# Value products of a two-layer mixer: operands built on chip from both parts of x, values kept on chip, layer 1's value sums made in layer 0, residual rows finished late

## The chip, the core and the metric

The kernel runs on one core of a Trainium2 chip. The metric is the device time of one execution in microseconds, as the median of several runs. The engines named below each work through a queue of their own in order: PE (TensorE) multiplies matrices, DVE (VectorE) and ACT (ScalarE) work elementwise, POOL (GpSimd) does elementwise work and issues DMAs, SP (SyncE) only issues DMAs.

## What is computed

Two layers of one mixer. Each layer projects x (512 tokens by 2048) with one wide weight matrix, runs three groups of attention heads, multiplies each group's output with a gate, projects back and normalises.

```python
def hybrid_layer(x, mem, w_in, b_forget, w_mem_kv, w_out, ln_gain, ln_bias):
    h = jnp.einsum('bsd,dn->bsn', x, w_in)
    (fq, fk, fv, fg, f_logit, dq, dk, dv, dg, iq, ik, iw, mq, mg) = jnp.split(h, offsets, axis=-1)
    log_f = jax.nn.log_sigmoid(f_logit + b_forget)
    y_fox = fox_attention(heads(fq), heads(fk), heads(fv), jnp.cumsum(log_f, axis=1)) * silu(fg)
    y_dsa = dsa_attention(rope(heads(dq)), rope(heads(dk)), heads(dv), rope(iq), rope(ik), iw) * silu(dg)
    k_mem, v_mem = jnp.split(jnp.einsum('bmd,dn->bmn', mem, w_mem_kv), 2, axis=-1)
    y_mem = memory_attention(heads(mq), k_mem, v_mem) * silu(mg)
    y = jnp.einsum('bsn,nd->bsd', jnp.concatenate([y_fox, y_dsa, y_mem], axis=-1), w_out)
    return layer_norm(ALPHA * x + y, ln_gain, ln_bias)      # x of the next layer

def reference(x, ...):
    for l in range(2):
        x = hybrid_layer(x, mem, w_in[l], ...)
    return x
```

There are 6 fox heads, 6 sparse (dsa) heads and 4 memory heads of width 128. The values fv and dv together are 1536 columns.

## The kernel before

All matrix products are made in float32r with every operand split in a high and a low part (`split`: ACT rounds the high part, DVE subtracts it to get the low part), and each product is three matmuls: high by high, low by high, high by low (`product`, L198 to L200).

**The weight stream.** The weights are a list of chunks of 1 MB (`wall`). One chunk after another is loaded by SP into one of three buffers `raw` (`load_w`, L214), split by halves into `whi` and `wlo` (`split_w`, three half chunks ahead of PE), and used by PE. A chunk is 48 matmuls of 512 columns for most kinds, and 24 of them for a chunk of the memory projection or of a value product. The load of chunk i+2 stands in SP's queue at the start of chunk i, behind all that was written into that queue before.

**Order.** The main loop goes over the chunks: memory values (mv), memory keys (mk), queries and gates of the memory heads (mq, mg), values, small columns, indexer queries, then per head gate, query and key, the third column block of the values (val, j = 2) between the fox and the dsa heads, and the output projection. All other work is written as generators: `begin(gen)` starts one, and `tick()` lets each running generator write its next piece, twice per chunk. What a generator writes stands in the engines' queues at that place.

**Values.** The first two thirds of the value columns, and the output projection, are made as a 2 by 2 block product with 7 instead of 8 block products (`PRODUCTS`, `VAL_ORDER`: P1, P2, Q6, P7, Q5, Q4, Q3). Their right operands are weight blocks or sums of them, T1 to T4. These sums are made in device memory by POOL's DMAs, copies and accumulating copies of 1 MB (`weight_sums`), sixteen DMAs for the values of one layer; before each, DVE writes a mark that POOL reads (`pool_waits`), so that the DMA is issued at the place in time at which it is written. The left operands are blocks of x or sums of them, S1 to S4: block (t, kh) is token half t and half kh of the 2048 inputs. Before the change they are made from x in device memory: `load_vx` has SP load twenty 256 KB blocks per layer (from `xt_in` for layer 0; for layer 1 from `xt_d`, into which `next_x` has SP store the new x, L783), DVE adds or subtracts 512 columns at once, and `val_operand` splits the sum at once. The finished values (`val_out`) are stored to device memory by SP (`v_d`, L724), eight tiles per layer for j = 0 and 1, and loaded again at head 0 and 4 (`load_v`, L729).

**Between the layers.** `next_x` normalises the sixteen tiles z (DVE), transposes them (PE, L779), scales and splits them (ACT L781 and L784; DVE and POOL L786). That runs beside mv and mk of layer 1. Later it has POOL multiply each z with the gain row, add the bias row and store the tile to `x1_d` as the residual of layer 1 (L796 to L798), beside the memory heads of layer 1.

**Buffers.** One pool of 69 tiles of 128 by 512 holds nearly everything else (`slot`), and PSUM has 8 banks.

Of the kernel before, what the change touches and what calls it, by code (L numbers as in the profile page):

```python
# [150 lines left out]
def kernel(  # L151
# [156 lines left out]
    def weight_sums(kind, l, pairs, names, pause):  # L308
# [4 lines left out]
        for name in names:  # L313
            for n, step in enumerate(steps[name]):
                for pair, g in every:
# [11 lines left out]
                    yield pause  # L327

    crow_d = [dram.tile([H_FOX, SEQ], F32, name=f"crow{l}") for l in range(DEPTH)]
    x1_d = dram.tile([SEQ, DM], F32, name="x1")  # L330
    v_d = {(j, st): dram.tile([P, 512], F32, name=f"v{j}{st}") for j in range(2) for st in range(4)}
    xt_d = dram.tile([P, KT * SEQ], F32, name="xt1")
# [336 lines left out]
    def val_operands(l):  # L669
        first = ((0, 0), (1, 0), (1, 1))  # L670
        load_vx(l, 0, *first)
        yield 1
        for i in range(4):
            if i < 3:
                load_vx(l, i + 1, *first)
            a11, a21, a22 = (vx.pop((*b, i)) for b in first)
            nc.vector.tensor_tensor(a21, a11, a21, op=ALU.subtract)
            nc.vector.tensor_tensor(a22, a21, a22, op=ALU.add)
            vx["S3", i], vx["S2", i] = a21, a22
            yield 1  # L680
            val_operand("S2", i, a22)
            yield 1
        for i in range(4):
            load_vx(l, i, (0, 0))
            val_operand("S3", i, vx.pop(("S3", i)))
            yield 1
        for i in range(4):
            load_vx(l, i, (0, 1))
            t = vx.pop((0, 0, i))
            nc.vector.tensor_tensor(t, t, vx["S2", i], op=ALU.subtract)  # L690
            val_operand("S1", i, t)
            yield 1
        for i in range(4):
            t = vx.pop((0, 1, i))
            nc.vector.tensor_tensor(t, t, vx.pop(("S2", i)), op=ALU.subtract)
            val_operand("S4", i, t)
            yield 2
# [10 lines left out]
    def val_out(name, ps):  # L708

        if name in ("P1", "P7", "Q6"):  # L710
# [44 lines left out]

    def load_rows(l):
        for c in range(4):
            for name, src in (("g", gain), ("b", bias)):
                t = slot("row")
                nc.gpsimd.dma_start(t, bass.AP(tensor=src.tensor,  # L760
                                               offset=src.offset + l * DM + c * 512,
                                               ap=[[0, P], [1, 512]]))
                rows[name, c] = t
# [4 lines left out]
    def next_x():  # L768
# [6 lines left out]
        for k in range(KT):  # L775
# [7 lines left out]
            nc.sync.dma_start(xt_d[:, k * SEQ:(k + 1) * SEQ], xf)  # L783
# [6 lines left out]
        yield 6  # L790
        load_rows(0)
        yield 2
# [7 lines left out]
        rows.clear()  # L800
# [71 lines left out]
    for i, (kind, l, j, col, _) in enumerate(chunks):  # L872
# [130 lines left out]
        elif kind == "val" and col == 3:  # L1003
            for st in range(4):
                vraw[j, st] = slot("vraw")
                nc.scalar.activation(vraw[j, st], out_ps[st], AF.Copy)
# [32 lines left out]
        if i == (8 if l == 0 else first[l]):  # L1039
            begin(weight_sums("val", l, range(1), ("T1", "T2", "T3", "T4"), 1 + l))  # L1040
        if kind == "mg" and j == H_MEM - 2:
            begin(val_operands(l))
        if kind == "small":
            chains.clear()
            begin(weight_sums("out", l, range(2), ("T1", "T3", "T2", "T4"), 2))
        if kind in ("fk", "dk"):
            n = j if kind == "fk" else H_FOX + j
            if n % 4 == 0:
                begin(split_v(n // 4))
        if kind == "fq" and j % 4 == 0:  # L1050
# [100 lines left out]
```

## Time and profile before

| what | value |
|---|---|
| median of 3 runs (lowest, highest) | 2005.66 us (2003.26, 2006.2) |
| the profiled execution's own time | 2005.69 us |
| its span from the first to the last instruction | 2003.9 us |
| mean granted TensorE clock | 0.994 |
| busy: PE, DVE, ACT, POOL | 1960.8, 1340.5, 780.5, 276.0 us |
| bytes read and written in device memory | 367.02 MB, 119.56 MB |

The profile is read from the whole to the part: the share of each engine, then what the bound engine waited for and where, then the queues of the engines that it waited for. A row of waits reads: engine, tile and line that waited, what released it, and then the total in us, the number of waits and the longest. A row of a timeline reads: start in us, duration in us, engine, line, operation, tiles, and in brackets the idle time before it and what ended that. Where several equal instructions are merged, x gives their number.

### The profile page before, as it was taken

How to read it: one execution, taken by the hardware profiler on the slowest of the kernel's cores; microseconds unless marked ns; L12 is line 12 of the kernel's file. 1: busy time of each engine (PE TensorE's matmuls, PEld its weight loads, DVE VectorE, ACT ScalarE, POOL GpSimd, SP SyncE). 2: the span in 40 equal slices, each digit the busy share in tenths (PEclk: the TensorE clock that was granted, in tenths of full speed). 3: DMA queues.
4: the chain of work that ended last, by engine and by line, in shares of the span. 5: the costliest groups of instructions: out<-in, count | busy, mean ns of one | idle time of the engine just before them, and what ended most of it. 6: DMA issues, size and time to landing. Idle time of an engine off the chain costs nothing. (4 is left out here: it accounts for less than half of the span.)

```text
span 2003.9 us, 24622 instructions
## 1 busy us (share of the span) xinstructions
PE 1960.8 (98%) x9410; PEld 1662.9 (83%) x9410; DVE 1340.5 (67%) x2205; ACT 780.5 (39%) x1232; POOL 276.0 (14%) x447
## 2 busy tenths in 40 slices
PE   9999999999999999999979999999999999999997
PEld 8887798888888888888868877988888888888886
DVE  6447577667864566788835675776678745657888
ACT  6334334433322332445453343344333223324453
POOL 0110011121110000100135610111221100001101
PEclk9999999999999999999989999999999999999999
DMA  9797559555664222466498974595656652224766
GB/s 368 242 300 234 200 197 269 165 167 178 169 193 143 85 84 84 163 221 228 160 299 294 263 252 176 213 266 163 181 168 179 183 144 92 77 83 168 279 208 154
DMA packets 72305, 385.41 MB, mean 192 GB/s; under 512 B 8688, under 2 KB 18928, under 8 KB 37884
## 3 DMA queue, kind: packets, MB, share of 16 engines
q1 hardware_dynamic: 57116, 262.18, 36.3%
q0 software_dynamic: 15072, 121.67, 23.4%
q8 instruction: 73, 1.20, 0.2%
q14 instruction: 44, 0.36, 0.1%
HBM read 367.02 MB, written 119.56 MB: 243 GB/s over the span
## 5 line engine op out<-in xcount | busy, mean ns | idle before, releaser
L192 DVE TENSOR_TENSOR wlo<-raw,whi 128x1024 fp32r<-128x1024 f32 (+1 forms) x425 | 523.0, 1236 | 244.7 <-ACT whi L191 243.3
L198 PE MATMUL c<-xh,whi 128*128 128x512 f32 (+1 forms) x1696 | 650.2, 383 | 0.4 <-ACT whi L191 0.4
L200 PE MATMUL c<-xh,wlo 128*128 128x512 f32 (+1 forms) x1696 | 647.0, 382 | 0.5 <-DVE wlo L192 0.5
L199 PE MATMUL c<-xl,whi 128*128 128x512 f32 (+1 forms) x1696 | 646.5, 381 | 0.0
L191 ACT ACTIVATE whi<-raw 128x1024 fp32r<-128x1024 f32 (+1 forms) x425 | 443.4, 1052 | 314.4 <-PE z L200 74.0
L200 PEld LDWEIGHTS c<-xh,wlo 128*128 128x128 f32 x1696 | 318.3, 188 | 57.9 <-DVE wlo L192 1.0
L198 PEld LDWEIGHTS c<-xh,whi 128*128 128x128 f32 x1696 | 318.5, 188 | 55.8 <-ACT whi L191 0.8
L199 PEld LDWEIGHTS c<-xl,whi 128*128 128x128 f32 x1696 | 318.6, 188 | 55.0
L199 PE MATMUL z<-wlo,yh 128*128 128x512 f32 (+1 forms) x434 | 167.8, 387 | 1.2 <-DVE wlo L192 1.2
L198 PE MATMUL z<-whi,yh 128*128 128x512 f32 (+1 forms) x434 | 167.9, 387 | 0.0
L200 PE MATMUL z<-whi,yl 128*128 128x512 f32 (+1 forms) x434 | 167.6, 386 | 0.0
L306 POOL TENSOR_TENSOR seen<-mark,mhalf 128x1 f32<-128x1 f32 x96 | 31.1, 323 | 863.8 <-DVE mark L305 759.9
L199 PEld LDWEIGHTS z<-wlo,yh 128*128 128x128 f32 x434 | 81.5, 188 | 18.2 <-DVE wlo L192 2.1
L198 PEld LDWEIGHTS z<-whi,yh 128*128 128x128 f32 x434 | 81.5, 188 | 16.4
L200 PEld LDWEIGHTS z<-whi,yl 128*128 128x128 f32 x434 | 81.5, 188 | 16.4
L198 PE MATMUL v<-whi,xh 128*128 128x512 f32 x224 | 87.6, 391 | 0.0
L191 ACT ACTIVATE qh<-rope 128x512 fp32r<-128x512 f32 x24 | 15.2, 633 | 185.1 <-DVE rope L427 185.1
L200 PE MATMUL v<-whi,xl 128*128 128x512 f32 x224 | 87.2, 389 | 0.0
L199 PE MATMUL v<-wlo,xh 128*128 128x512 f32 x224 | 87.2, 389 | 0.0
L191 ACT ACTIVATE qh<-c 128x512 fp32r<-128x512 f32 x32 | 19.2, 598 | 146.8 <-PE c L200 141.9
L191 ACT ACTIVATE pth<-pt 128x512 fp32r<-128x512 f32 (+1 forms) x72 | 35.3, 526 | 100.5 <-PE pt L590 98.6
L424 DVE TENSOR_TENSOR rope<-c,tabs 128x512 f32<-128x512 f32 (+2 forms) x42 | 26.8, 639 | 69.0 <-PE c L200 68.7
(193 smaller groups left out, 2697.1 us busy)
## 6 DMA issues: line engine op xcount, KB each, us to landing
raw<-in_wall_dram SPq DMA_DIRECT2D x163, 1024.0 KB, 7.1
sum<-in_wall_dram POOLq DMA_DIRECT2D x48, 1024.0 KB, 8.9
raw<-sum SPq DMA_DIRECT2D x48, 1024.0 KB, 5.0
vx<-in_xt_dram SPq DMA_DIRECT2D x20, 256.0 KB, 11.0
vx<-xt SPq DMA_DIRECT2D x20, 256.0 KB, 6.7
memraw<-in_memt_dram SPq DMA_DIRECT2D x16, 256.0 KB, 5.9
xraw<-in_xt_dram SPq DMA_DIRECT2D x16, 256.0 KB, 9.1
v<-vraw SPq DMA_DIRECT2D x16, 256.0 KB, 2.2
```

The source lines that it names most:

```text
L191: nc.scalar.activation(hi, src, AF.Copy)
L192: nc.vector.tensor_tensor(lo, src, hi.bitcast(F32), op=ALU.subtract)
L198: nc.tensor.matmul(ps, ah, bh, start=start, stop=False, skip_group_check=more)
L199: nc.tensor.matmul(ps, ah, bl, start=False, stop=False, skip_group_check=more)
L200: nc.tensor.matmul(ps, al, bh, start=False, stop=stop, skip_group_check=more)
L306: nc.gpsimd.tensor_tensor(seen, mark, mhalf, op=ALU.mult)
L424: nc.vector.tensor_tensor(t1[:rows, c], ps[:rows, c], cos[:rows, c], op=ALU.mult)
```

## The change

The left operands of the value products are now made from the parts of x that are on chip already, the tiles `xh` and `xl` (`val_sum`): a sum of two blocks is the two high parts and the two low parts, added one after another on DVE in pieces of 256 columns, 80 instructions for one layer. `val_operand` writes the high part, and the low part only at the next tick. The sums S1 and S2 are made from mq 0 on; S3 beyond the first tile waits until P1 is done, the splits of S1 until Q6 is done, those of S4 until P7 is done. `load_vx`, the store of x in `next_x` and `xt_d` are gone. The values of j = 0 and 1 stay on chip; those of j = 2 are stored and loaded instead (at dk 2), and `split_v(1)` begins at fq 4, one chunk earlier. The value sums of layer 1 follow the output sums of layer 0 in one generator (`sums_ahead`), and the value sums of layer 0 have longer pauses. `next_x` stores z as it is, and `residual_rows` reads each tile again, finishes it on POOL and stores it, beside the third value block and the first dsa heads of layer 1.

```diff
@@ load_w
-            src = wall[key] if kind == "wall" else sums.pop(key)
+            src = wall[key] if kind == "wall" else sums[key]
@@ weight_sums
-                    yield pause
+                    yield next(pauses) if pauses else 2
+    def value_sums(l, pauses=None):
+        return weight_sums("val", l, range(1), ("T1", "T2", "T3", "T4"), pauses)
+    def sums_ahead(l):
+        yield from weight_sums("out", l, range(2), ("T1", "T3", "T2", "T4"))
+        if l + 1 < DEPTH:
+            yield from value_sums(l + 1)
@@ the left operands
-    def load_vx(l, i, *blocks):
-        src = (xt_in if l == 0 else xt_d).rearrange("p (k t c) -> p k t c", k=KT, t=2)
-        for t, kh in blocks:
-            vx[t, kh, i] = slot("vx")
-            nc.sync.dma_start(vx[t, kh, i].rearrange("p (k c) -> p k c", k=2),
-                              src[:, 8 * kh + 2 * i:8 * kh + 2 * i + 2, t, :])
-    def val_operand(name, i, x):
-        vleft[name, i] = slot("vxh", F32R), slot("vxl", F32R)
-        split(x, *vleft[name, i])
...
+    def x_block(t, kh, i, e, part):
+        return xT[8 * kh + 2 * i + e][part].bitcast(F32)[:, t * 256:(t + 1) * 256]
+    def val_sum(name, i, terms, into=None):
+        sums = {t: vx.get((t, i), into) for t, _, _ in terms if isinstance(t, str)}
+        dst = vx[name, i] = into or slot("vx")
+        for e in range(2):
+            d = dst[:, e * 256:(e + 1) * 256]
+            halves = [sums[t][:, e * 256:(e + 1) * 256] if isinstance(t, str)
+                      else x_block(*t, i, e, h) for t, h, _ in terms]
+            acc, signs = halves[0], [op for _, _, op in terms]
+            for x, op in zip(halves[1:], signs[1:]):
+                nc.vector.tensor_tensor(d, acc, x, op=op)
+                acc = d
+    def val_operand(name, i):
+        x = vx[name, i]
+        hi, lo = vleft[name, i] = slot("vxh", F32R), slot("vxl", F32R)
+        nc.scalar.activation(hi, x, AF.Copy)
+        yield 1
+        nc.vector.tensor_tensor(lo, x, hi.bitcast(F32), op=ALU.subtract)
+    def val_operands():
+        for i in range(4):
+            val_sum("S1", i, ((a21, 0, add), (a22, 0, sub), (a21, 1, add), (a22, 1, sub)))
+            yield 1
+            val_sum("S2", i, ((a11, 0, add), ("S1", 0, sub), (a11, 1, add)))
+            yield 1
+        for i in range(4):
+            yield from val_operand("S2", i)
+            val_sum("S4", i, ((a12, 0, add), ("S2", 0, sub), (a12, 1, add)), vx.pop(("S2", i)))
+            yield 1
+            if i:
+                yield from wait_for("P1")
+            val_sum("S3", i, ((a11, 0, add), (a21, 0, sub), (a11, 1, add), (a21, 1, sub)))
+            yield from val_operand("S3", i)
+            del vx["S3", i]
+        for name, product in (("S1", "Q6"), ("S4", "P7")):
+            yield from wait_for(product)
+            for i in range(4):
+                yield from val_operand(name, i)
+                del vx[name, i]
@@ val_out: the values stay in vraw
-        for key in [k for k in vraw if k[0] in (0, 1)]:
-            nc.sync.dma_start(v_d[key], vraw.pop(key))
-    def load_v(j):
-        for st in range(4):
-            vraw[j, st] = slot("vraw")
-            nc.sync.dma_start(vraw[j, st], v_d[j, st])
@@ next_x
-            nc.sync.dma_start(xt_d[:, k * SEQ:(k + 1) * SEQ], xf)
...
-        yield 6
-        load_rows(0)
-        yield 2
         for c in range(4):
             for st in range(4):
-                t = z.pop((st, c))
-                nc.gpsimd.tensor_tensor(t, t, rows["g", c], op=ALU.mult)
-                nc.gpsimd.tensor_tensor(t, t, rows["b", c], op=ALU.add)
-                nc.gpsimd.dma_start(x1_d[st * P:(st + 1) * P, c * 512:(c + 1) * 512], t)
-            yield 4
+                nc.gpsimd.dma_start(x1_d[st * P:(st + 1) * P, c * 512:(c + 1) * 512], z.pop((st, c)))
+                if st % 2:
+                    yield 1
+    def residual_rows(l):
...
+                t[n] = slot("z")
+                nc.gpsimd.dma_start(t[n], x1_d[st * P:(st + 1) * P, c * 512:(c + 1) * 512])
...
+                nc.gpsimd.tensor_tensor(d, d, rows["g", c], op=ALU.mult)
+                nc.gpsimd.tensor_tensor(d, d, rows["b", c], op=ALU.add)
+                nc.gpsimd.dma_start(x1_d[st * P:(st + 1) * P, c * 512:(c + 1) * 512], d)
...
+            yield 1 + n % 2
@@ main loop
-        if i == (8 if l == 0 else first[l]):
-            begin(weight_sums("val", l, range(1), ("T1", "T2", "T3", "T4"), 1 + l))
-        if kind == "mg" and j == H_MEM - 2:
-            begin(val_operands(l))
+        if i == 8:
+            begin(value_sums(l, iter([1, 2] * 6 + [2] * 4)))
+        if kind == "mq" and j == 0:
+            begin(val_operands())
...
+        if kind == "val" and j == 2 and col == 0 and l > 0:
+            begin(residual_rows(l))
+        if kind == "dk" and j == 2:
+            for st in range(4):
+                vraw[2, st] = slot("vraw")
+                nc.sync.dma_start(vraw[2, st], v_d[st])
+            begin(split_v(2), 1)
```

PE's queue holds the same instructions in the same order before and after. Three queues change.

SP between the layers, before: `xt` is `xt_d`, `xf` a tile of the new x, `raw` a weight buffer.

```order
L783 DMA xt_168<-xf_8510 128x512
L783 DMA xt_168<-xf_8522 128x512
L214 DMA raw_8535<-in_wall_dram 128x2048
L783 DMA xt_168<-xf_8558 128x512
L783 DMA xt_168<-xf_8570 128x512
L783 DMA xt_168<-xf_8598 128x512
L783 DMA xt_168<-xf_8610 128x512
L214 DMA raw_8622<-in_wall_dram 128x2048
```

The same stretch of SP's queue after the change:

```order
L214 DMA raw_8526<-in_wall_dram 128x2048
L214 DMA raw_8568<-in_wall_dram 128x2048
L214 DMA raw_8628<-in_wall_dram 128x2048
L214 DMA raw_8706<-in_wall_dram 128x2048
L214 DMA raw_8793<-in_wall_dram 128x2048
```

The sixteen stores of the new x have left the queue, and each weight load stands behind a weight load.

SP in the value products Q4 and Q3 of layer 0, before: `v` is `v_d`, `sum` a weight sum.

```order
L214 DMA raw_1914<-sum_1355 128x2048
L214 DMA raw_1953<-sum_1414 128x2048
L724 DMA v_166<-vraw_1910 128x512
L724 DMA v_167<-vraw_1912 128x512
L214 DMA raw_1996<-in_wall_dram 128x2048
L214 DMA raw_2030<-in_wall_dram 128x2048
L724 DMA v_162<-vraw_1821 128x512
L724 DMA v_163<-vraw_1823 128x512
```

The same stretch after the change:

```order
L214 DMA raw_1940<-sum_1607 128x2048
L214 DMA raw_1982<-sum_1681 128x2048
L214 DMA raw_2023<-in_wall_dram 128x2048
L214 DMA raw_2057<-in_wall_dram 128x2048
L214 DMA raw_2093<-in_wall_dram 128x2048
```

The value stores, and further up the loads of x, are gone here too.

DVE in the value products of layer 0, before, in Q6 and P7: `vx` is an operand sum, `vxl` its low part.

```order
L192 TENSOR_TENSOR wlo_1735<-raw_1669,whi_1734 128x1024
L690 TENSOR_TENSOR vx_1641<-vx_1641,vx_1273 128x512
L192 TENSOR_TENSOR vxl_1754<-vx_1641,vxh_1753 128x512
L192 TENSOR_TENSOR wlo_1758<-raw_1732,whi_1757 128x1024
L690 TENSOR_TENSOR vx_1663<-vx_1663,vx_1315 128x512
L192 TENSOR_TENSOR vxl_1777<-vx_1663,vxh_1776 128x512
```

DVE after the change, in P2 of layer 0, where it has the most to do (line 678 of the changed file is `val_sum`, 687 is `val_operand`):

```order
L678 TENSOR_TENSOR vx_1000<-xh_670,vx_1000 128x256
L678 TENSOR_TENSOR vx_1000<-vx_1000,xl_671 128x256
L678 TENSOR_TENSOR vx_1000<-xh_674,vx_1000 128x256
L678 TENSOR_TENSOR vx_1000<-vx_1000,xl_675 128x256
L192 TENSOR_TENSOR wlo_1691<-raw_1639,whi_1690 128x1024
L678 TENSOR_TENSOR vx_1706<-xh_511 128x256
L678 TENSOR_TENSOR vx_1706<-vx_1706,xl_512 128x256 x2
L678 TENSOR_TENSOR vx_1706<-xh_515 128x256
L678 TENSOR_TENSOR vx_1706<-vx_1706,xl_516 128x256 x2
L192 TENSOR_TENSOR wlo_1717<-raw_1688,whi_1716 128x1024
```

One long subtraction with its low part per half chunk has become four or six short ones, no longer followed at once by a low part that waits for ACT.

## Rows read from the trace of the kernel before

**Rows 1.** The page: busy time of each engine, its share and instructions.

```profile
PE 1960.8 (98%) x9410; PEld 1662.9 (83%) x9410; DVE 1340.5 (67%) x2205; ACT 780.5 (39%) x1232; POOL 276.0 (14%) x447
```

**Rows 2.** What PE waited for, whole span: total us, times, longest.

```profile
PE c L198 <- ACT whi L191: 9.1, 3, 6.4
PE v L199 <- DVE wlo L192: 6.7, 13, 0.8
...
PE pt L590 <- DVE bt L582: 2.3, 2, 1.1
```

**Rows 3.** Windows of 10 us: PE, PEld, DVE, ACT, POOL busy; PEclk, DMA, GB/s.

```profile
1040.00:1050.00 10.00, 3.17 (x21) 2.68 (x20) 1.56 (x2) 2.35 (x3) 0.00 (x0) 0.81 0.96 335
```

**Rows 4.** PE's timeline: the first matmuls of the stages around the values and the layers.

```profile
29.96 0.28 PE L198 MATMUL c<-memh,whi 128*128 128x256 f32 x1
...
52.99 0.40 PE L198 MATMUL c<-xh,whi 128*128 128x512 f32 x1
...
152.66 0.40 PE L198 MATMUL v<-whi,xh 128*128 128x512 f32 x1
...
163.57 0.27 PE L408 MATMUL ptm<-ident,pm 128*128 128x128 f32 x1
...
176.70 0.39 PE L198 MATMUL v<-whi,vxh 128*128 128x512 f32 x1
...
238.16 0.50 PE L198 MATMUL c<-xh,whi 128*128 128x512 f32 x1 [0.42 <-ACT whi L191]
...
985.77 0.39 PE L198 MATMUL v<-whi,memh 128*128 128x512 f32 x1
...
996.65 1.03 PE L779 MATMUL xt<-ident,z 128*128 128x128 f32 x8
1000.27 1.04 PE L779 MATMUL xt<-ident,z 128*128 128x128 f32 x8
...
1056.70 0.40 PE L198 MATMUL c<-xh,whi 128*128 128x512 f32 x1
...
1180.40 0.39 PE L198 MATMUL v<-whi,vxh 128*128 128x512 f32 x1
...
1242.86 0.39 PE L198 MATMUL c<-xh,whi 128*128 128x512 f32 x1
```

**Rows 5.** SP's timeline between the layers.

```profile
1001.72 10.83 SPq L783 DMA_DIRECT2D xt<-xf  x4
1012.65 1.34 SPq L214 DMA_DIRECT2D raw<-in_wall_dram  x1
```

**Rows 6.** ACT's timeline there: the split that waits for the load of 1012.65.

```profile
1019.53 1.06 ACT L191 ACTIVATE whi<-raw 128x1024 fp32r<-128x1024 f32 x1 [3.23 <-DMA raw<-in_wall_dram]
```

**Rows 7.** SP's timeline in the value products of layer 0.

```profile
218.15 0.92 SPq L724 DMA_DIRECT2D v<-vraw  x2
219.17 0.91 SPq L214 DMA_DIRECT2D raw<-in_wall_dram  x2
```

**Rows 8.** ACT's timeline there: the split that waits for the loads of 219.17.

```profile
224.40 2.01 ACT L191 ACTIVATE whi<-raw 128x1024 fp32r<-128x1024 f32 x2 [7.19 <-DMA raw<-in_wall_dram]
```

**Rows 9.** DVE's timeline there: low part of an operand, then low part of the weights.

```profile
193.78 0.69 DVE L192 TENSOR_TENSOR vxl<-vx,vxh 128x512 fp32r<-128x512 f32 x1 [0.70 <-ACT vxh L191]
194.73 1.23 DVE L192 TENSOR_TENSOR wlo<-raw,whi 128x1024 fp32r<-128x1024 f32 x1 [0.26 <-ACT whi L191]
```

**Rows 10.** Groups of DVE by form, whole span: count, busy us, mean ns of one.

```profile
L192 DVE TENSOR_TENSOR wlo<-raw,whi 128x1024 fp32r<-128x1024 f32 x421 | 520.3, 1242 | 237.8 <-ACT whi L191 236.4
L377 DVE SCALAR_TENSOR_TENSOR y<-po,tanh 128x256 f32<-128x256 f32 x64 | 24.1, 418 | 45.7 <-PE po L200 45.7
```

**Rows 11.** Groups of POOL and of DVE between 1075 and 1165 us.

```profile
L797 POOL TENSOR_TENSOR z<-z,row 128x512 f32<-128x512 f32 x16 | 25.0, 1563 | 1.7 <-DMA row<-in_bias_dram 0.6
L192 DVE TENSOR_TENSOR wlo<-raw,whi 128x1024 fp32r<-128x1024 f32 x15 | 25.2, 1693 | 8.8 <-ACT whi L191 8.8
```

**Rows 12.** DMA issues between 60 and 160 us: count, KB, median us to landing.

```profile
sum<-in_wall_dram POOLq DMA_DIRECT2D x8, 1024.0 KB, 10.4
```

More of the change, by code (lines that the diff above doesn't have):

```diff
@@ L306, in pool_waits, with weight_sums @@
         nc.gpsimd.tensor_tensor(seen, mark, mhalf, op=ALU.mult)
[L308 removed]
+    def weight_sums(kind, l, pairs, names, pauses=None):
         every = [(pair, g) for pair in pairs for g in range(2)]
@@ L326, in weight_sums @@
                         nc.gpsimd.dma_start(sums[key], src)
-                    yield pause
+                    yield next(pauses) if pauses else 2
[5 more added lines that the diff above has]
+            yield from value_sums(l + 1)
     crow_d = [dram.tile([H_FOX, SEQ], F32, name=f"crow{l}") for l in range(DEPTH)]
+    v_d = [dram.tile([P, 512], F32, name=f"v{st}") for st in range(4)]
     x1_d = dram.tile([SEQ, DM], F32, name="x1")
-    v_d = {(j, st): dram.tile([P, 512], F32, name=f"v{j}{st}") for j in range(2) for st in range(4)}
-    xt_d = dram.tile([P, KT * SEQ], F32, name="xt1")
     active = []
@@ L699, in val_left, with wait_for @@
+            val_sum("S3", i, ((a11, 0, add), (a21, 0, sub), (a11, 1, add), (a21, 1, sub)))
[6 more added lines that the diff above has]
+                del vx[name, i]
+    val_done = []
+    def wait_for(name):
+        while name not in val_done:
+            yield 1
     def val_left(name, i, e, st):
@@ L754, with load_row @@
     rows = {}
+    def load_row(l, c):
+        for name, src in (("g", gain), ("b", bias)):
+            t = rows[name, c] = slot("row")
+            nc.gpsimd.dma_start(t, bass.AP(tensor=src.tensor, offset=src.offset + l * DM + c * 512,
+                                           ap=[[0, P], [1, 512]]))
     def load_rows(l):
         for c in range(4):
[L758 to L763, printed above, removed]
+            load_row(l, c)
     def normalise(st, c, mv, rs):
@@ L789, in next_x @@
                 yield 1
[L790 to L792 removed]
         for c in range(4):
             for st in range(4):
[L795 to L800 removed]
+                nc.gpsimd.dma_start(x1_d[st * P:(st + 1) * P, c * 512:(c + 1) * 512], z.pop((st, c)))
+                if st % 2:
+                    yield 1
+    def residual_rows(l):
+        tiles = [(st, c) for c in range(4) for st in range(4)]
+        t = {}
+        for n in range(len(tiles) + 1):
+            if n < len(tiles):
+                st, c = tiles[n]
+                if st == 0:
+                    load_row(l - 1, c)
+                t[n] = slot("z")
+                nc.gpsimd.dma_start(t[n], x1_d[st * P:(st + 1) * P, c * 512:(c + 1) * 512])
+            if n:
+                st, c = tiles[n - 1]
+                d = t.pop(n - 1)
+                nc.gpsimd.tensor_tensor(d, d, rows["g", c], op=ALU.mult)
+                nc.gpsimd.tensor_tensor(d, d, rows["b", c], op=ALU.add)
+                nc.gpsimd.dma_start(x1_d[st * P:(st + 1) * P, c * 512:(c + 1) * 512], d)
+                if st == 3:
+                    del rows["g", c], rows["b", c]
+            yield 1 + n % 2
     terms = {}
@@ L1037 @@
             begin(attend(l, kind[0], j), 1, whole=True)
-        if i == (8 if l == 0 else first[l]):
-            begin(weight_sums("val", l, range(1), ("T1", "T2", "T3", "T4"), 1 + l))
-        if kind == "mg" and j == H_MEM - 2:
-            begin(val_operands(l))
+        if i == 8:
+            begin(value_sums(l, iter([1, 2] * 6 + [2] * 4)))
+        if kind == "mq" and j == 0:
+            begin(val_operands())
         if kind == "small":
             chains.clear()
[L1045 to L1050, printed above, removed]
-            load_v(j // 4)
+            val_done.clear()
+            begin(sums_ahead(l))
+        if kind == "fk" and j == 0:
+            begin(split_v(0))
+        if kind == "fq" and j == 4:
+            begin(split_v(1))
+        if kind == "val" and j == 2 and col == 0 and l > 0:
[5 more added lines that the diff above has]
+            begin(split_v(2), 1)
         if kind == "fq":
```

31 lines of the change are left out of this document (8 added, 23 removed).

## Prediction

> **What bounds the kernel.** I read the page first. PE is busy for 1960.8 us of a span of 2003.9 us [rows 1], and PE's instructions and their order stay the same. So the change can only win what PE loses, and it can only lose by making PE wait anew. The list of what PE waited for comes second [rows 2]: most is for the splits of the weights, by ACT (9.1 us in 3 waits) or DVE (6.7 us in 13). These are not waits for arithmetic as such, so the third view is PE's timeline by stage, which tells where they lie. I compare each stage with the same work done undisturbed.
>
> P1 of layer 0 takes 163.57 - 152.66 = 10.91 us for 48 matmuls [rows 4]. The last five value products should then take 54.55 us. They take 238.16 - 176.70 = 61.46 us in layer 0 and 1242.86 - 1180.40 = 62.46 us in layer 1 [rows 4], 6.9 and 7.9 us too many.
>
> Between the layers, from the first mv matmul at 985.77 to the first mq matmul at 1056.70, PE takes 70.93 us [rows 4]. The undisturbed work is: mv, 96 matmuls, 2 x 10.91 = 21.82 us; mk, as in layer 0, 52.99 - 29.96 = 23.03 us; eight groups of eight transposes. From one group to the next it is 1000.27 - 996.65 = 3.62 us, of which twelve matmuls take 10.91 / 4 = 2.73, so a group costs 0.89 us and eight cost 7.1. That makes 51.95 us, and 19.0 us are lost. [...]
>
> The fourth view tells why: SP's queue. Between the layers SP stands for 10.83 us over four stores of xt, each of which must wait for an xf that PE has yet to transpose and ACT has yet to scale, and only then issues a weight load, at 1012.65 [rows 5]. ACT gets those weights at 1019.53, after 3.23 us of idling [rows 6]. Two further rounds are like it. In the value products the stores of v do the same: SP waits until DVE has finished the values, issues the stores at 218.15 and the weight loads only at 219.17 [rows 7]; ACT idles 7.19 us until 224.40 [rows 8]. Between these, DVE and ACT wait for each other in turn: the low part of an operand waits 0.70 us for its high part, and the low part of the weights stands behind it [rows 9].
>
> **The change, part by part.** The terms go against the profiled execution's own 2005.69 us, which lies at the median of 2005.66.
>
> 1. Stores of x gone from SP's queue. A weight load then waits only for a free buffer, that is for the last split of the chunk three before. A raw buffer is refilled about two and a half chunks ahead of PE, so the stalls of this stretch should go: 19.0 us at most. I take 18.0; the upper end leaves 1 us for DVE's normalisation, which delays the splits there, and the lower end is in the second rival. POOL's sixteen stores of z to x1 come in their stead, but in POOL's queue, which no weight load shares, and after the last transposes. The sixteen DMAs for sums and the 32 POOL instructions on residual rows leave this stretch or the memory heads behind it, which also takes load off the DMA engines (0.96 busy in [rows 3]).
>
> 2. Loads of x and stores of v gone from SP's queue in both layers, and the splits of operands no longer back to back with their sums: 6.9 + 7.9 = 14.8 us at most. I take 6.5 + 7.5 = 14.0.
>
> 3. More DVE work. 16 sums of 512 columns, at the 0.69 us of such an instruction [rows 9], were 11.0 us for a layer. Now it is 80 of 256 columns. The nearest row of that width is 418 ns [rows 10], so 33.4 us, 22.4 us more. 54 of the 80 lie beside mq and mg, where a chunk takes PE at least 10.91 us and the splits of weights take DVE 2 x 1.24 [rows 10], which hides them. The tight place is P2 and Q6, 21.8 us of PE: eight splits of weights (9.9 us), 26 short sums (10.9), five low parts of operands (3.4), and six other instructions of 256 or 512 columns for the values and the last memory head (3.6 us at most), by the same rows: 27.8 us. DVE falls behind by about 6 us. The weights are split three half chunks ahead, 3 x 2.73 = 8.2 us, so I expect this to be caught up in P7, where only low parts remain. Cost: from 0 to 5 us a layer; I take 0.5 each, since the lead covers it.
>
> 4. Value sums of layer 1 in layer 0, beside dsa heads, where POOL does nothing else: nothing. In layer 0 the pauses are longer, so that six of the sixteen DMAs now run beside the value products (third term of the slower case below): nothing.
>
> 5. Values of j = 0 and 1 kept on chip: eight more tiles are held until the first fox heads. In the indexer the tiles for the scores then come free just before they are taken again, so ACT may wait for DVE there. 0 to 2 us a layer; I take 0.5 each. The stores and loads of the third block stand in SP's queue at val j = 2 and dk 2, where a chunk takes PE 10.91 us and the loads have two chunks of lead: nothing.
>
> 6. `split_v(1)` one chunk earlier. Its four low parts (0.69 us each, [rows 9]) leave the softmax of fox head 4. There PE waits twice, once a layer, 2.3 us in all, for the scaled probabilities [rows 2]. I take 2.0 of the 2.3.
>
> 7. Residual rows beside val j = 2 and the first dsa heads of layer 1. Where POOL did this before, the split of the weights took DVE 1693 ns instead of 1242 [rows 10, 11], and PE did not wait. A head has a softmax whose time decides when PE can transpose: 0 to 3 us in each of four heads; I take 0.5 in all.
>
> Sum: 18.0 + 14.0 + 2.0 - 1.0 - 1.0 - 0.5 = 31.5 us, and 2005.7 - 31.5 = 1974.2, in round numbers **1974 us**. With every stall gone and nothing new it would be 19.0 + 14.8 + 2.3 = 36.1 us, 1969.6.
>
> **The rivals.**
>
> DVE becomes the bound of the value products (0.13). If the short sums take as long as the long ones, because each waits for the one before it, 26 of them cost 7 us more in P2 and Q6, the 6 us of arrears become 13, more than the lead of 8.2, and the gain of part 2 is halved: 7 us back, about 1981; with all of it gone, 1988. For it: the six sums of a tile form chains in place. Against it: time to catch up from P7 on.
>
> The weights stay late between the layers (0.08). The DMA engines are 0.96 busy there [rows 3], and 4 MB of z go out in the place of 4 MB of x. If that, not the queue, delays the loads, half of part 1 is lost: 9 us, 1983. Against it: the load of 1012.65 was issued late and then took under 7 us [rows 5, 6].
>
> POOL holds DVE up in the dsa heads (0.04). A POOL instruction of 1563 ns [rows 11] that stops DVE in each link of a softmax costs 3 us a head, 12 us for four heads: 1986. [...]
>
> Slower than before (0.02). The weights of Q4 in layer 0 are T4, whose last DMA is now issued in Q6 instead of ahead of P1. SP's queue waits for it, and every weight load stands behind it. With 10.4 us to landing [rows 12] it is there some 12 us before PE needs it. Each microsecond beyond these 12 stops PE for one, so the kernel becomes slower than before only if that DMA lands over 12 + 32 = 44 us late, at four times the measured time: 2006 and more.
>
> It changes nothing (0.02): the stalls have another cause that stays, 2004 to 2008.
>
> **How the numbers follow.** My forecast, 1970 to 1980, has 0.71. The rivals take 0.13, 0.08, 0.04, 0.02 and 0.02. The range of 8 in 10 goes from 1969, where no stall is left, to 1986, which takes in the first half of the DVE case and the other two. What a measurement of this kernel can tell from no change is about 0.2%, 4 us. So faster 0.96, the same 0.02, slower 0.02.
>
> **What would show it.** In the profile after: SP's queue between 985 and 1050 us holds weight loads alone; the first mq matmul of layer 1 comes 52 to 54 us after the first mv matmul, with the granted clock at 1.00 throughout; the five products Q6 to Q3 take 54.6 to 56 us in both layers; the waits of the c and v matmuls for splits fall from 15.8 us to under 3. I am wrong if DVE is busy without a gap from P2 to P7 while PE waits for the low parts, if the weight loads between the layers land later than 9 us after their issue, or if PE waits for probabilities in the first dsa heads of layer 1.

## The result and the profile after

The changed kernel takes **1976.11 us** (median of 4 runs, 1975.2 to 1976.65) against 2004.93 us for the kernel before, measured beside it (4 runs, 2003.26 to 2006.2). The ratio is 0.9856, with a 95% interval of 0.9839 to 0.9873. The profiled execution took 1976.65 us, its span is 1974.9 us, its mean granted clock 0.996. 359 MB are read and 117 MB written.

The page, as in [rows 1], and the list of what PE waited for over the whole span, as in [rows 2] (total us, times, longest):

```profile
PE 1953.2 (99%) x9410; PEld 1661.7 (84%) x9410; DVE 1375.7 (70%) x2333; ACT 780.9 (40%) x1232; POOL 291.2 (15%) x479
```

```profile
PE v L198 <- ACT whi L191: 3.0, 4, 1.3
PE v L199 <- DVE wlo L192: 2.0, 4, 0.8
...
PE ix L523 <- ACT rel L528: 0.9, 2, 0.5
PE cqt L486 <- DVE crow L481: 0.8, 2, 0.4
PE c L200 <- DVE wlo L192: 0.3, 1, 0.3
```

The long waits of the c matmuls for `whi` (9.1 us in 3 waits) are gone, the waits of the v matmuls for `wlo` fell from 6.7 us in 13 waits to 2.0 in 4, and the row for `pt` has disappeared. DVE is 35 us busier. PE's timeline, at the same places as [rows 4]:

```profile
177.61 0.39 PE L198 MATMUL v<-whi,vxh 128*128 128x512 f32 x1
...
236.28 0.39 PE L198 MATMUL c<-xh,whi 128*128 128x512 f32 x1
...
981.03 0.39 PE L198 MATMUL v<-whi,memh 128*128 128x512 f32 x1
...
1033.43 0.40 PE L198 MATMUL c<-xh,whi 128*128 128x512 f32 x1
...
1157.25 0.39 PE L198 MATMUL v<-whi,vxh 128*128 128x512 f32 x1
...
1215.65 0.39 PE L198 MATMUL c<-xh,whi 128*128 128x512 f32 x1
```

Together with the rows of before these cut the span into seven stretches (us), whose differences make up the whole 29.0 us of the two spans (2003.9 and 1974.9):

| stretch | before | after | gain |
|---|---|---|---|
| start to Q6 of layer 0 | 176.70 | 177.61 | -0.91 |
| Q6 to Q3, layer 0 | 61.46 | 58.67 | 2.79 |
| rest of layer 0 | 747.61 | 744.75 | 2.86 |
| first mv to first mq matmul | 70.93 | 52.40 | 18.53 |
| mq to the end of P2, layer 1 | 123.70 | 123.82 | -0.12 |
| Q6 to Q3, layer 1 | 62.46 | 58.40 | 4.06 |
| rest of layer 1 | 761.04 | 759.25 | 1.79 |

Between the layers SP's queue now holds weight loads alone. The first row below is SP's timeline, in the place of [rows 5]; the second is a window of 10 us in the same stretch, in the place of [rows 3] (busy PE, PEld, DVE, ACT, POOL, granted clock, DMA share, GB/s):

```profile
974.47 75.39 SPq L214 DMA_DIRECT2D raw<-in_wall_dram  x12
```

```profile
1020.00:1030.00 10.00, 10.00 (x85) 10.00 (x85) 3.73 (x5) 4.83 (x7) 1.96 (x3) 1.00 0.30 107
```

PE is busy for the whole of this window, at a granted clock of 1.00. ACT's waits for weights between 975 and 1075 us, of which [rows 6] showed one, fell from 13.0 us in 3 to 4.2 in 1 (before, then after):

```profile
ACT whi L191 <- DMA raw<-in_wall_dram: 13.0, 3, 5.3
```

```profile
ACT whi L191 <- DMA raw<-in_wall_dram: 4.2, 1, 4.2
```

In the value products SP holds loads alone as well, with no store where [rows 7] had one. Of the short sums (line 678) most take 425 ns, close to the 418 ns of [rows 10]; the columns are the least, median and greatest duration in ns and the first and last start:

```profile
L678 DVE TENSOR_TENSOR vx<-vx,xl x96: 424/425/428, 66.8 to 1170.0; 128x256 f32<-128x256 f32 x96
```

**A new stall.** The value products gained 6.85 us, less than half of the 14.8 that the prediction held possible. PE stops once in each layer, ahead of the second half chunk of P7. In layer 1 ACT waits for no DMA there, so it is read in that layer. PE's timeline, then ACT's, then DVE's:

```profile
1170.62 0.39 PE L200 MATMUL v<-whi,vxl 128*128 128x512 f32 x1
1172.07 0.49 PE L198 MATMUL v<-whi,vxh 128*128 128x512 f32 x1 [1.06 <-ACT whi L191]
1173.33 0.50 PE L199 MATMUL v<-wlo,vxh 128*128 128x512 f32 x1 [0.76 <-DVE wlo L192]
1173.66 0.41 PE L200 MATMUL v<-whi,vxl 128*128 128x512 f32 x1
1173.89 0.61 PE L198 MATMUL v<-whi,vxh 128*128 128x512 f32 x1
```

```profile
1158.01 0.63 ACT L685 ACTIVATE vxh<-vx 128x512 fp32r<-128x512 f32 x1 [6.24 <-DVE vx L678]
...
1170.44 0.63 ACT L685 ACTIVATE vxh<-vx 128x512 fp32r<-128x512 f32 x1 [8.43 <-DVE vx L678]
1170.97 1.99 ACT L191 ACTIVATE whi<-raw 128x1024 fp32r<-128x1024 f32 x2
```

```profile
1159.62 1.23 DVE L192 TENSOR_TENSOR wlo<-raw,whi 128x1024 fp32r<-128x1024 f32 x1 [1.65 <-ACT whi L191]
...
1169.52 0.88 DVE L678 TENSOR_TENSOR vx<-vx,xl 128x256 f32<-128x256 f32 x2
1172.05 1.23 DVE L192 TENSOR_TENSOR wlo<-raw,whi 128x1024 fp32r<-128x1024 f32 x1 [1.64 <-ACT whi L191]
```

These are to be read together. ACT stands for 8.43 us before the high part of S3's operand, since DVE has yet to make its six sums. Behind that high part in ACT's queue stands the high part of the weights (`whi`, 1170.97), and the low part of the weights (1172.05) waits on DVE for that. PE idles for 1.2 and 1.0 us more than a matmul needs (10.91 / 48 = 0.23 us from one start to the next), and from 1173.89 on eight matmuls take 0.61 to 0.63 us each in place of 0.39: the granted clock is 0.50 from 1174 to 1176 us and 0.83 from 1170 to 1180. Waits of about 2.2 us and the slower matmuls behind them together cost 4.0 (58.40 us against the 54.40 of e1, below).

The sums are chains in place, and the rows of DVE's timeline show what a chain costs. Behind a sum at 1165.08 the one that reads its result starts at 1165.54, 0.46 us later; the next, which needs neither, starts at 1165.88, 0.34 later. All 96 sums of the row above start 0.45 to 0.46 us behind the one that they need. So waiting for the sum before costs about 0.1 us, and a short sum does not take as long as a long one (0.69 us), which was the first rival's condition.

### The profile page after: what moved, and what is told of

It reads as the page before. It is cut to its first block, busy times and chain, and to the rows that moved or that the text cites. A ratio compares the mean times of both kernels' runs of the same rounds, so it can differ in the third digit from the quotient of the medians.

```text
span 1974.9 us, 24601 instructions
## 1 busy us (share of the span) xinstructions
PE 1953.2 (99%) x9410; PEld 1661.7 (84%) x9410; DVE 1375.7 (70%) x2333; ACT 780.9 (40%) x1232; POOL 291.2 (15%) x479
## 4 chain that ended last, share of the span: by engine, by line
PE 93%; DVE 4%; issue 1%; ACT 1%; DMA 0%; POOL 0%; SPq 0%; POOLq 0%; ACTq 0%; DVEq 0%
PE c L198 19%; PE c L200 19%; PE c L199 19%; PE z L199 5%; PE z L200 5%; PE z L198 5%; PE v L199 4%; PE v L200 4%; PE v L198 4%; PE pt L597 1%; DVE wlo L192 1%; PE po L200 1%; PE po L199 1%; PE ix L523 1%; PE po L198 1%
```

## Experiments

The times of the stretches are read from PE's timeline as above. Most are edits of the changed kernel; e8 builds on e1, e9 and e10 build on e8, and e11 is an edit of the kernel before.

### e1: the chain at S3

```diff
-        for i in range(4):
-            yield from val_operand("S2", i)
...
-            yield from val_operand("S3", i)
...
+        for i in range(5):
+            if i < 4:
+                high("S2", i)
             if i:
...
+                high("S3", i - 1)
+            yield 1
+            if i:
+                low("S3", i - 1)
...
```

`high` and `low` are the two parts of `val_operand`, on ACT and on DVE. Both parts of S3 are written one half chunk later, beside those of the next S2.

> Edit, against the changed kernel: the high part of S3's operand, which ACT makes, is written one half chunk after the sums on which it depends, beside the high part of the next S2; the low parts go with it. DVE has the same instructions, only in a slightly other order. Theory 1 (a chain: ACT stands before the high part of S3 while DVE makes the six sums, and the high part of the weights for P7 stands behind it): no wait of PE before the second half chunk of P7 in either layer, Q6 to Q3 fall from 58.7 and 58.4 us to about 54.6 to 55.5, together 6.5 to 8 us, so about 1968 to 1970 us. Theory 2 (DVE simply has more work from P2 to P7 than the lead covers): PE then waits for the low part of the weights in the place of the high part, the stages stay at 57.5 us or more, and the time stays at 1974 to 1976 us.

Measured: 1969.88 us (1969.3 to 1970.88), ratio to before 0.9822 (0.9808 to 0.9837). Q6 to Q3 take 55.73 us in layer 0 and 54.40 in layer 1, where no wait of PE is left. ACT's timeline in layer 1, now with the weights ahead of the operand that waits:

```profile
1159.86 1.06 ACT L191 ACTIVATE whi<-raw 128x1024 fp32r<-128x1024 f32 x1 [1.67 <-PE v L200]
1164.50 0.63 ACT L705 ACTIVATE vxh<-vx 128x512 fp32r<-128x512 f32 x1 [3.58 <-DVE vx L678]
```

DVE makes the same instructions, 2333 in both. So what stalled PE was the place of that high part in ACT's queue; the amount of DVE's work alone does not stall it. The low parts moved too, but DVE had not waited for a high part of S3 in the changed kernel: between 1130 and 1175 us its waits for ACT's parts are for those of the weights (4.8 us in 3) and of a memory head (1.2). Theory 1 holds; in layer 0 1.3 us are left over.

### e8: the pauses of the value sums of layer 0

```diff
-            begin(value_sums(l, iter([1, 2] * 6 + [2] * 4)))
+            begin(value_sums(l, iter([1] * 16)))
```

> Edit, against e1_high_later: the value sums of layer 0 have pauses of one tick again, as in the kernel before, so that the last of the sixteen is issued before the value products and not beside them. In e1_high_later Q6 to Q3 of layer 0 still take 1.3 us more than those of layer 1, and ACT waits up to 7.5 us for a load of a sum there. Theory 1 (the longer pauses, which put six sums beside the value products, cost that 1.3 us): Q6 to Q3 of layer 0 fall from 55.7 to 54.4 us, 1968.5 to 1969 us. Theory 2 (the sums then come while x, the tables and the weights of the memory heads are loaded, and delay these): PE waits in the memory heads of layer 0, 1 to 6 us more, 1970 to 1975 us.

Measured: **1968.32 us** (1967.7 to 1968.46), ratio 0.9814 (0.9799 to 0.9828). Q6 to Q3 take 54.40 us in layer 0 and 54.39 in layer 1, the undisturbed time. ACT's waits for a load of a sum between 150 and 240 us fall from 11.9 us in e1 to 2.0. Theory 1 holds. This is the fastest version measured; of the changed kernel's 1976.11 us it takes off 7.8.

### e2, e3, e6, e7, e11, e12: what the stall between the layers was made of

Five edits of the changed kernel put back, one at a time or together, what the change took away: the sixteen stores of the new x (in SP's queue or in POOL's), and the sums of layer 1 beside them. The sixth, e11, is one line of the kernel before: its stores of the new x go into POOL's queue.

```diff
+            nc.sync.dma_start(xt_d[:, k * SEQ:(k + 1) * SEQ], xf)     # e2, e7; e3, e11, e12: nc.gpsimd
...
-        if l + 1 < DEPTH:                                             # e6, e7, e12
-            yield from value_sums(l + 1)
...
+        if l > 0 and i == first[l]:                                   # e6, e7, e12
+            begin(value_sums(l))
```

> Edit, against the changed kernel: the sixteen stores of the new x between the layers are put back, each in SP's queue right behind the scaling of its tile, as in the kernel before; nobody reads what they store. Theory 1 (SP's order of issue made the stall between the layers): the stretch from the first mv matmul to the first mq matmul grows from 52.4 us to 68 to 71 us and the kernel takes about 1992 to 1995 us. Theory 2 (the stall was load on the DMA engines and on POOL, which the moved value sums and residual rows have taken away): the stretch stays below 56 us and the time at 1976 to 1980 us.

> Edit, against the changed kernel: the same sixteen stores of the new x as in e2_xt_sp, but issued in POOL's queue, which holds no weight load. The same bytes at the same places. Theory 1 (order in the queue): no stall comes back, the stretch between the layers takes 52.4 to 54 us, 1976 to 1978 us. Theory 2 (bytes: the DMA engines are the limit there, and the weight loads get their turn late): the stretch grows by 9 us or more, as in e2_xt_sp, 1985 to 1995 us.

> Edit, against the changed kernel: the value sums of layer 1 are made at the start of layer 1 again, beside mv, mk and the memory heads, as in the kernel before; no stores of the new x. With the stores back alone the stretch between the layers grew by 9.4 us, which is half of what the change won there. Theory 1 (the sums load the DMA engines, and that costs only where the weight loads are issued late, so not here): the stretch from the first mv to the first mq matmul takes 52.4 to 54.5 us, the time is 1976 to 1978 us. Theory 2 (the sums cost the other half by themselves): the stretch takes 60 us or more, 1984 to 1986 us.

> Edit, against the changed kernel: the stores of the new x back in SP's queue and the value sums of layer 1 back at the start of layer 1, both together. Theory 1 (late issue and busy DMA engines act on the same loads, each late load also lands later): the stretch takes 68 to 72 us, as in the kernel before, 1992 to 1996 us, whatever the sums cost alone. Theory 2 (the sums have no part in it, and the other half came from something else that was moved, as the residual rows on POOL): the stretch takes 61 to 63 us, 1984 to 1987 us.

> Edit, against the kernel before and in one line: the stores of the new x between the layers are issued in POOL's queue instead of SP's; everything else, the value sums beside them too, stays. Theory 1 (the order in SP's queue is the condition, and the traffic of the sums only multiplies what it costs): nearly the whole 18.5 us come back by this line, the stretch from the first mv to the first mq matmul takes 53 to 57 us, 1988 to 1992 us. Theory 2 (order and traffic each have their own half): only about 9 us, the stretch takes 60 to 63 us, 1995 to 1998 us.

> Edit, against the changed kernel: the stores of the new x back, in POOL's queue as in e3_xt_pool (stretch 54.7 us), and the value sums of layer 1 back beside them as in e6_sums_l1 (52.4 us). With the kernel before as the base, the same pair took 69.7 us, and there ACT waited to write the scaled x until earlier stores had landed: the tiles that they hold came free too late. Theory 1 (a store holds a tile until it lands, and beside the sums in POOL's queue it lands late; neither alone costs much): the stretch takes 64 to 71 us, ACT waits for stores of x, 1987 to 1994 us. Theory 2 (what kept the stall alive with the kernel before as the base is something else that the change moved, as the finishing of the rows): the stretch takes 54 to 57 us, 1976 to 1979 us.

Measured, the stretch from the first mv to the first mq matmul in us, and the median time of the kernel:

| stores of x | without the sums | with the sums |
|---|---|---|
| none | 52.40 (the changed kernel, 1976.11) | 52.40 (e6, 1975.05) |
| in POOL's queue | 54.67 (e3, 1974.63) | 70.67 (e12, 1994.16) |
| in SP's queue | 61.82 (e2, 1984.61) | 70.70 (e7, 1993.1) |

With the kernel before as the base, e11 (POOL's queue, with the sums) takes 69.68 us of its 70.93, and the time is the same: 2004.11 us, ratio 0.9994 (0.9985 to 1.0003). So my expectation for e2 (68 to 71 us) was too high, and both of those for e11 fell (nearly the whole gain by one line, or half of it). By their stretches e6, e7 and e12 came out as their theory 1, and e3 as well, but for 0.7 us more than expected there. The sums alone cost nothing. The stores alone cost 9.4 us in SP's queue and 2.3 in POOL's. Both together cost 18.3, whichever queue the stores are in. The time of e3 is below that of the changed kernel although its stretch is longer: in its profile the value products took 1.6 us less in either layer, by the stall of e1, which varies (see e5).

Two kinds of wait of ACT tell why. In e2 there are waits for weights, since SP issues a load only behind four stores that wait for their tiles to be written, and one wait for a tile that a store still holds; the rows are SP's timeline and ACT's waits between 975 and 1075 us:

```profile
997.18 6.96 SPq L803 DMA_DIRECT2D xt<-xf  x4
1004.24 0.38 SPq L214 DMA_DIRECT2D raw<-in_wall_dram  x1
```

```profile
ACT whi L191 <- DMA raw<-in_wall_dram: 5.6, 3, 2.1
ACT xh L804 <- DMA xt<-xf: 4.6, 1, 4.6
```

In e12 no weight load is held back. ACT waits there to write the next scaled x, and what releases it is the landing of an earlier store, whose tile it takes over (the same waits, then one of them on ACT's timeline):

```profile
ACT xf L799 <- DMA xt<-xf: 16.9, 3, 9.0
```

```profile
1024.68 0.78 ACT L799 ACTIVATE xf<-xt,gcol 128x512 f32<-128x512 f32 x1 [8.95 <-DMA xt<-xf]
```

Each store holds a tile of the pool until it lands, and between 975 and 1075 us it lands after a median of 5.8 us in e3 and 10.2 us in e12, where POOL's queue and the DMA engines also carry the sums. ACT stands, and the high parts of the weights stand behind it. In e7 both kinds are there, 12.2 us for weights and 8.0 for tiles. That the tiles ran out is read from these releases; a larger pool was not tried.

### e5: the splits of the second column block

```diff
-        if kind == "fq" and j == 4:
+        if kind == "fk" and j == 4:
             begin(split_v(1))
```

> Edit, against the changed kernel: the splits of the second column block of values begin at fk 4 again, as in the kernel before, one chunk later. Theory 1 (their four low parts stood in DVE's queue ahead of the scaling in the softmax of fox head 4): PE waits for probabilities in that head again, once a layer, 2.0 to 2.6 us in all, 1978 to 1979 us. Theory 2 (the wait went because values and their loads left the queues, not for the place of the splits): no such wait, 1976 us within 0.5.

Measured: 1977.07 us (1975.94 to 1978.53), ratio 0.9858 (0.9843 to 0.9874). The wait is back, in the waits of PE over the whole span:

```profile
PE pt L597 <- DVE bt L589: 2.3, 2, 1.2
```

The rests of the two layers grow by 1.5 and 1.1 us, as theory 1 has it. The median grows by 1.0 only: in the profiled execution Q6 to Q3 took 57.34 and 56.79 us, less than in the changed kernel. That stall varies. In the profiles of seven kernels with the same value products (the changed one, e2, e3, e5, e6, e7, e12) these products take 57.0 to 59.3 us in layer 0 and 56.8 to 58.4 in layer 1.

### e4 and e10: the stores of the values

```diff
+        for key in [k for k in vraw if k[0] in (0, 1)]:
+            nc.sync.dma_start(vs_d[key], vraw.pop(key))
...
+        if kind == "fq" and j in (0, 3):
+            load_v(j // 3)
```

> Edit, against the changed kernel: the eight values of the column blocks 0 and 1 are again stored by SP as soon as they are made (end of Q5, Q4 and Q3) and loaded again at fox heads 0 and 3. Theory 1 (a good part of the loss in the value products of the kernel before came from these stores, since SP waits at each for DVE's last subtraction and the weight loads stand behind it): Q6 to Q3 grow by 2 to 6 us a layer, 1980 to 1988 us. Theory 2 (the loss was that of the loads of x and of the splits written back to back with their sums; the stores alone come late enough to be hidden by the two chunks of lead): less than 0.5 us a layer, 1976 to 1977 us.

> Edit, against e8_high_later_short_pauses: the eight values of the column blocks 0 and 1 are stored by SP as soon as they are made and loaded again at fox heads 0 and 3, as in e4_v_stored. In the changed kernel this cost 3.8 us, of which about 2 and 0.6 us lay in Q6 to Q3 of the two layers, 0.6 us behind them. Theory 1 (the price is SP's: each store waits for DVE's last subtraction and holds the weight loads behind it, whatever else stalls): again 2 to 4 us, 1970 to 1972.5 us. Theory 2 (a store only cost something because the splits were already late; with the stall gone the two chunks of lead hide it): below 0.7 us, 1968 to 1969 us.

Measured: e4, on the changed kernel, 1979.88 us (1979.3 to 1980.44), 3.8 more; Q6 to Q3 take 60.67 and 58.95 us. e10, on e8, 1968.85 us (1968.43 to 1969.35), 0.5 more; 54.42 and 54.83. So the price of these stores hangs on another stall. In e4 the first two, behind P2, wait for DVE's addition, which is late in the chain of S3. SP's timeline of e4 in layer 1 and the split of ACT that waits for the load behind:

```profile
1163.97 0.92 SPq L748 DMA_DIRECT2D vs<-vraw  x2
1165.00 20.18 SPq L214 DMA_DIRECT2D raw<-sum  x6
```

```profile
1170.28 1.06 ACT L191 ACTIVATE whi<-raw 128x1024 fp32r<-128x1024 f32 x1 [6.72 <-DMA raw<-sum]
```

That store is issued 4.2 us after Q6 began (1159.75); in e10 it is 1.4 us (1154.41 against 1153.04), and the loads are in time. Theory 2 holds for e10. For e4 theory 1 holds in kind: Q6 to Q3 grew by 2.0 us in layer 0, but by 0.6 in layer 1, less than the 2 to 6 of the expectation.

### e9: the residual rows beside the memory heads

```diff
-        if kind == "val" and j == 2 and col == 0 and l > 0:
+        if kind == "mq" and j == 1 and l > 0:
             begin(residual_rows(l))
```

> Edit, against e8_high_later_short_pauses: POOL finishes the residual rows of layer 1 beside the memory heads (from mq 1 on) instead of beside the third value block and the dsa heads. There the split of a half chunk of weights took DVE 1693 ns beside POOL in the kernel before, against a mean of 1242, and DVE now also makes 54 short sums there. Theory 1 (a chunk of PE, 10.91 us, covers all of it, so the place of the rows is worth nothing): 1968 to 1969 us, no new wait of PE. Theory 2 (with the short sums DVE has no slack left there; it comes into the value products in arrears): PE waits for splits in the memory heads or in P1 to Q6, 2 to 8 us more, 1970 to 1976 us.

Measured: 1984.62 us (1983.6 to 1985.22), 16.3 us more than e8 and twice the most that I expected. The stretch from Q6 to Q3 of layer 1 takes 69.86 us in place of 54.39. PE's waits there, then a window in it (columns as above):

```profile
PE v L199 <- DVE wlo L192: 8.4, 3, 5.0
PE v L200 <- DVE vxl L701: 2.8, 1, 2.8
```

```profile
1170.00:1180.00 10.00, 4.18 (x17) 2.77 (x16) 9.83 (x10) 0.66 (x2) 8.35 (x9) 1.00 0.28 86
```

DVE is busy for 9.83 of 10 us and does ten instructions. The groups of DVE by form between 1128 and 1180 us (count, busy us, mean ns), of e8 and then of e9:

```profile
L192 DVE TENSOR_TENSOR wlo<-raw,whi 128x1024 fp32r<-128x1024 f32 x18 | 21.9, 1221 | 5.5 <-ACT whi L191 5.5
L678 DVE TENSOR_TENSOR vx<-vx,xl 128x256 f32<-128x256 f32 x16 | 6.8, 425 | 0.5
...
L678 DVE TENSOR_TENSOR vx<-xh 128x256 f32<-128x256 f32 x6 | 2.5, 418 | 0.0
...
L397 DVE TENSOR_REDUCE nm<-sm 128x2 f32<-128x512 f32 x2 | 1.4, 692 | 0.0
```

```profile
L192 DVE TENSOR_TENSOR wlo<-raw,whi 128x1024 fp32r<-128x1024 f32 x11 | 14.7, 1356 | 0.5 <-ACT whi L191 0.5
L678 DVE TENSOR_TENSOR vx<-vx,xl 128x256 f32<-128x256 f32 x16 | 12.2, 762 | 0.6
L678 DVE TENSOR_TENSOR vx<-xh 128x256 f32<-128x256 f32 x6 | 7.8, 1301 | 0.0
L701 DVE TENSOR_TENSOR vxl<-vx,vxh 128x512 fp32r<-128x512 f32 x4 | 6.9, 1737 | 0.0
...
L397 DVE TENSOR_REDUCE nm<-sm 128x2 f32<-128x512 f32 x2 | 1.4, 692 | 0.0
```

The short sums of one group take three times as long in the mean, 1301 ns in place of 418, while the reduction keeps its time. Over the instructions that e9 makes there, the longer means add up to 17 us of DVE in these 52 us. ACT waits for no DMA between 1130 and 1230 us, so late weights are not the cause. Theory 2 holds in kind.

## Why the prediction was right, and where not

**The sum.** 1974 us was predicted and 1976.1 measured, faster as forecast. That it came so close is luck in part: the value products brought 6.2 us less than taken, the rests of the two layers 4.2 us more (4.65 in place of 0.5). Of the signs that were named, SP's queue with loads alone, the 52 to 54 us between the layers (52.40) and the clock of 1.00 there came. The 54.6 to 56 us for Q6 to Q3 did not. The two kinds of wait that make up the 15.8 us fell to 2.0, but other waits of the c and v matmuls for splits, which that sum left out, make it 5.3 in all.

**Part 1, the stretch between the layers: right in size, half right in its cause.** 18.0 was taken and 18.5 came. But SP's queue alone, which I named as the cause, is worth at most 9.4 us (e2), and 2.3 of these come in POOL's queue as well (e3). The stores hurt in two ways, by holding back loads in an in-order queue and by holding tiles until they land. To move them into POOL's queue, where no weight load stands, would have gained about 1 us of the stretch as long as the sums run beside it (e11), and no measurable time. The gain came since they are gone. The second rival, weights late for the load on the DMA engines, stands in so far as the sums double the price; it did not come to pass because nothing is left for them to delay (e6).

**Parts 2 and 3, the value products: the mis-sized term.** 14.0 less 1.0 was taken, 2.79 + 4.06 = 6.85 came. The step that failed is in part 3: "from 0 to 5 us a layer; I take 0.5 each, since the lead covers it". Against the undisturbed 54.40 the cost was 4.3 and 4.0, near the upper end; of the 4.3, 1.3 belong to part 4. In the seven profiles named at e5 it lies between 2.4 and 4.9. The count of DVE's work was not at fault: the short sums take 425 ns where 418 were assumed, and with the same sums e1 has no stall in layer 1, so the lead of three half chunks does cover the arrears. What I left out was the place of the new instructions in ACT's queue, though [rows 9] had shown me DVE and ACT waiting for each other in turn. A high part that waits for DVE stood ahead of a split of the weights, DVE's next split waited for that one, and in each of two rounds DVE lost 1.65 us to waiting (1159.62 and 1172.05). The first rival foresaw the place, the sign and about the size (half of part 2), though by DVE's throughput alone; what stopped PE was the alternation. How the 14.8 us of the kernel before divide between the loads of x, the stores of v and the splits behind their sums is not shown: the stores alone cost 3.8 us (e4) or 0.5 (e10), the loads of x were not put back.

**Part 4: put at nothing, 1.3 us measured.** The earlier sums of layer 1 cost nothing (e6: 52.40 with and without). The longer pauses in layer 0 cost 1.3 us once S3's stall is gone (e1 against e8). The sums that were made beside the value products took a median of 12.5 us (four from the weights) and 14.6 us (two from another sum) to land (the changed kernel, 150 to 215 us), not the 10.4 of [rows 12].

**Part 5: 1.0 taken, nothing measured.** The indexer's wait is 0.9 us in two, the same as before. **Part 6: right.** The 2.3 us of waits for `pt` went, and came back when the splits were put back (e5).

**Part 7: 0.5 taken, and it holds where the rows are now.** No wait of PE is listed between 1500 and 1720 us. But the reason given, that PE did not wait for this in the place before either, would not have carried over: there DVE now makes the short sums, and the same rows cost 16 us (e9).

**What the sum left out:** 0.9 us in the chunk behind Q3 of layer 0 (16.01 to 15.07 us), whose weights are no longer late, and 1.1 us of waits for `cqt` (1.9 to 0.8), whose cause was not looked for. The 0.9 us lost ahead of Q6 of layer 0 are not the change's: they lie before the first mk matmul (30.87 in place of 29.96 us), which comes between 29.8 and 31.1 us in the profiles of all fourteen kernels.

## What to carry to other kernels

When a change makes one engine's instruction wait for another's, look at what stands behind it in the waiting engine's queue: the lead of a pipeline covers work, but two in-order queues that wait for each other in turn eat it up, and one tick between producer and consumer can be enough (e1: 6 us). A store can cost more than its bytes: here it held what was queued behind it (e2: ACT waited 5.6 us for weights) and the tile that it read (e12: 16.9 us), so another queue may only change which of the two bites, and a stall with two causes, each enough by itself, doesn't shrink until both are gone (here beside the sums: 70.70 us in e7 and 70.67 in e12 against 52.40 in e6). Where two engines' instructions lengthen each other, price them by their number, not only by their time (e9: 14 short sums of 0.42 us took 1.37 to 2.00).

## What the runs showed of the hardware

In e9 a short sum on DVE that ran beside a POOL instruction could take about the whole time of that instruction longer. DVE's timeline shows a sum of 0.41 us at 1139.89 and one of the same form that takes 1.78 at 1141.14; POOL's shows what runs beside the second:

```profile
1139.89 0.41 DVE L678 TENSOR_TENSOR vx<-xh 128x256 f32<-128x256 f32 x1
...
1141.14 1.78 DVE L678 TENSOR_TENSOR vx<-xh 128x256 f32<-128x256 f32 x1
```

```profile
1141.30 1.32 POOL L844 TENSOR_TENSOR z<-z,row 128x512 f32<-128x512 f32 x1
```

The long one takes about its own 0.42 us and POOL's 1.32 together. Of the 80 short sums of layer 1 in e9, 66 take 0.41 to 0.43 us, and 14 take 1.37 to 2.00, each of these beside a POOL instruction. So the means above are mixtures: a split of 1221 ns grew by 11%, the short sums by 65 to 211%, and a held short one loses 0.9 to 1.6 us, no more than about one POOL instruction (1.3 to 1.6). POOL's instructions were held too: one at 1132.98, while DVE makes three splits from 1133.15 on, takes 3.67 us in place of 1.3.

The reductions of DVE were not held. Two of them in e9, and the POOL instruction that the second lies wholly beside:

```profile
1128.18 1.41 DVE L397 TENSOR_REDUCE nm<-sm 128x2 f32<-128x512 f32 x2
```

```profile
1128.45 1.31 POOL L844 TENSOR_TENSOR z<-z,row 128x512 f32<-128x512 f32 x1
```

Each takes 0.69 us, as in e8. In the prediction I knew the price only as the mean over long splits (1693 ns in place of 1242, 451 more for each), which understates it for many short instructions.
